# When a planner makes weight chunks ready around a layer norm, and when it keeps still

## The chip, the cores and the metric

The kernel runs on one core of one Trainium2 chip. The metric is device time in microseconds (us) of one execution. The time before the change is 2328.68 us, the median of three runs (2328.07 to 2328.75).

The engines are called as the profile calls them: PE is TensorE, the matrix engine; DVE is VectorE; ACT is ScalarE; SP is the queue of SyncE, which in this kernel does nothing but issue DMAs.

## The reference

One decoder layer in float32: batch 1, 256 tokens, model width 2048. Cut to what matters:

```python
h = x
h = layer_norm(alpha*h + 0.5 * swiglu(h, w_ffn1_gu, w_ffn1_down), ln_g[0], ln_b[0])

rq, rk, rv, rg, aq, ak, av, gate_r, gate_a = split(h @ w_in)
ret_branch = (silu(rg) * head_group_norm(retention(rotary(rq), rotary(rk), rv))) @ w_ret_out
att_branch = sliding_window_attention(rotary(aq), rotary(ak), av, sinks) @ w_att_out
mixed = (sigmoid(gate_r) * ret_branch + sigmoid(gate_a) * att_branch) @ w_mix_out
h = layer_norm(alpha*h + mixed, ln_g[1], ln_b[1])

h = layer_norm(alpha*h + 0.5 * swiglu(h, w_ffn2_gu, w_ffn2_down), ln_g[2], ln_b[2])

ple = sigmoid(h @ w_ple_gate) * (p @ w_ple_proj)
h = layer_norm(alpha*h + ple, ln_g[3], ln_b[3])
```

`swiglu(h, gu, down)` is `(silu(g) * u) @ down` with `g, u = split(h @ gu)` and an inner width of 5632. A layer norm needs all 2048 columns of a token before its mean and variance are known, so nothing that follows it can begin before the product ahead of it has ended for that token.

## The kernel before

**Products.** Every large product takes a high and a low part of both operands (`Sum.add`, L279 to L288): low x high, high x high and high x low are three matmuls into one PSUM bank. The activations lie transposed, contraction index on the partitions, high and low part of all 256 tokens in one tile (`ht`). The 256 tokens are two halves, t = 0 and t = 1, of 128 each.

**Weights.** Weights come in chunks of 512 KB (`Chunk`, L93). A chunk is loaded by one DMA from SP (L104), ACT casts its high part (L90), and DVE subtracts to get the low part (L91). These two together are called a split. A unit of the plan is either a `Single`, one chunk with 12 matmuls (2 halves of the tokens x 2 blocks of the contraction x 3), or a `Seven`, two chunks used in a Strassen-like form with 21 matmuls. All these tiles, and most other temporary ones (the norm's vectors among them), live in one pool of 46 slots (`slots`, L54) of 4 KB for each partition. A tile that is asked for takes the place of an earlier one, and the instruction that writes it first waits until the earlier tile's last reader is done.

**The planner.** The order of the instructions on each engine is the order in which the program writes them. `plan` is the list of all units in the order of use. `fill` (L183) goes on as long as it may: it makes the next loaded unit ready (the split) while the units that are ready sum up to less than `ahead` matmuls (45), and loads the next unit of the plan while ready and loaded ones sum up to less than `far` (90). Both need room within the number of slots last set by `slots_for_weights`. `take` hands out the next ready unit, `done` gives its slots back and calls `fill`. So a split stands on ACT and DVE at the point where the program called `fill`, ahead of all that the program writes later.

**Around a norm.** Three layer norms (i = 0 after the first feed-forward block, tile `f1y`; i = 1 after the mixers, `mixy`; i = 2 after the second feed-forward block, `f2y`) are handled by the class `Norm` (L484):

- `Norm.run` (L520) queues the four loads of the norm's vectors `ln_g` and `ln_b` (`ln_vectors`, L446; each 1024 values given to all 128 partitions, 512 KB). For i < 2 it also loads and splits `praw`, the per-layer input, into `pt` (L525 to L528). It then calls `held_out`.
- `held_out` (L394) goes over the last chunks before the norm twice. In the first pass it takes each chunk and multiplies it with the tokens of t = 0 only, calls `fill`, and keeps the chunk. Then `normal(0)` (L499) is written: DVE adds the last columns to the residual (`columns`, L494, L835 or L1184), works out mean and variance (`ln_stats`, L457), and normalizes the first 512 columns (`ln_normal`, L464, with its two instructions L468 and L469). In the second pass the kept chunks are multiplied with t = 1 on PE, while DVE normalizes t = 0. The argument `between` says after how many half chunks of the second pass the four groups of transposes (`turn`, L509, `ln_turn`, L471, the matmuls of L476) are written: (8, 9, 11, 12) for all three norms. ACT and DVE then make high and low part of each transposed group in the new `ht`; at norm 1, where `keepers` names two groups, ACT first copies these to `keep`, and they are split from there. Six chunks are held (`HELD_PAIRS` = 3 pairs of two columns, or `HELD_MIX` = 6).
- `Norm.first` (L549) belongs to the product behind the norm. The first six chunks (`FRONT`) of its weights are multiplied with t = 0 of the new activations, and meanwhile DVE normalizes t = 1 and PE transposes it, one group after the second, third, fourth and sixth chunk. Then the same six chunks are multiplied with t = 1. For the last product, `w_pg`, the groups stand after the fourth, fifth and sixth chunk with t = 0 and the second with t = 1. `first` calls `fill` after each chunk (L562) as well.
- For i < 2, `put_by` (L583) stands between the two: the product `pp` of the per-layer input, which doesn't need the norm's output.

The product behind norm 0 is `w_rv` (retention values), behind norm 1 the second feed-forward block's `f2_gu`, behind norm 2 `w_pg`.

## Time and profile before

| what | value |
| --- | --- |
| median of 3 runs | 2328.68 us (2328.07 to 2328.75) |
| the profiled execution's own time | 2328.84 us |
| its span, first to last instruction | 2327.1 us |
| mean granted clock of TensorE | 0.995 |
| busy: PE / DVE / ACT / POOL | 2289.2 / 1828.9 / 1145.5 / 96.6 us |
| read from HBM | 455.43 MB, 199 GB/s over the span |

The busy time of an engine is the time in which at least one of its counted instructions was under way. The span and the busy times are of one execution, whose own time is 0.16 us over the median. Two further kinds of view are used below. A list in order of time shows each instruction with its start, duration, engine, line, operation, out and in tiles, and in brackets the idle time of its engine ahead of it with what released it. The list of waits sums these idle times by place and releaser. Tiles are named as in the program, so `lnps` is the PSUM bank of the transposes, `lw_rv` the low part of a `w_rv` chunk, and `rw_`, `hw_` are the raw and the high tile of the same chunk.

### The profile page before, as it was taken

The numbers are of one execution on the slowest core, as the hardware profiler recorded it, in microseconds if no ns is written. First come the engines' busy times: TensorE is split into PE (matmuls) and PEld (weight loads), VectorE is DVE, ScalarE is ACT, GpSimd is POOL, SyncE is SP. The second block draws the span as 40 slices with busy tenths as digits, with TensorE's granted clock in tenths as the row PEclk, the third lists the DMA queues.
The fourth block names the chain that finished last, engine by engine and source line by source line (L and its number), as shares of the span: only waits on it lengthen the run. The fifth ranks groups of instructions, "written<-read, shape, count | busy, mean of one in ns | idle before, by whom it ended". The sixth has DMA issues, their size and how long they took to land.

```text
span 2327.1 us, 28608 instructions
## 1 busy us (share of the span) xinstructions
PE 2289.2 (98%) x10532; PEld 1893.4 (81%) x10532; DVE 1828.9 (79%) x2288; ACT 1145.5 (49%) x1384; POOL 96.6 (4%) x53
## 2 busy tenths in 40 slices
PE   9999999999998999999999999999999999999987
PEld 7888888888887888888778888788888888888876
DVE  7998988988987874777554555769898899889766
ACT  5655555555553343434554443355455555655432
POOL 0000000000000530133000000000000000000000
PEclk9999999999999999999999999999999999999998
DMA  9555665665586564545445666566566666465851
GB/s 316 188 192 186 210 205 171 208 211 193 197 304 239 172 223 160 171 157 189 163 155 181 199 210 215 193 233 211 181 197 201 190 196 219 168 222 199 332 192 55
DMA packets 193725, 465.71 MB, mean 200 GB/s; under 512 B 14768, under 2 KB 16048, under 8 KB 193584
## 3 DMA queue, kind: packets, MB, share of 16 engines
q1 hardware_dynamic: 191456, 460.91, 58.8%
q10 hardware_dynamic: 2128, 2.97, 0.4%
q8 instruction: 83, 1.36, 0.2%
q14 instruction: 58, 0.48, 0.1%
HBM read 455.43 MB, written 8.39 MB: 199 GB/s over the span
## 4 chain that ended last, share of the span: by engine, by line
PE 95%; DVE 4%; DMA 1%; issue 0%; ACT 0%; DVEq 0%; ACTq 0%
PE f1g L286 3%; PE f1g L288 3%; PE f1g L287 3%; PE f2g L286 3%; PE f2g L288 3%; PE f2g L287 3%; PE gt L286 3%; PE f1u L286 3%; PE f1u L288 3%; PE f1u L287 3%; PE rqk L237 3%; PE f2u L287 3%; PE f2u L288 3%; PE f2u L286 3%; PE gt L287 3%; PE gt L288 3%
## 5 line engine op out<-in xcount | busy, mean ns | idle before, releaser
L91 DVE TENSOR_TENSOR lf_gu<-rf_gu,hf_gu 128x1024 fp32r<-128x1024 f32 (+1 forms) x293 | 347.2, 1214 | 23.5 <-ACT hf_gu L90 22.6
L90 ACT CAST hf_gu<-rf_gu 128x1024 fp32r<-128x1024 f32 (+1 forms) x293 | 292.1, 1045 | 16.4 <-DMA rf_gu<-in_f_gu 12.5
L91 DVE TENSOR_TENSOR lw_in_f<-rw_in_f,hw_in_f 128x1024 fp32r<-128x1024 f32 x148 | 208.1, 1438 | 61.8 <-ACT hw_in_f L90 59.2
L91 DVE TENSOR_TENSOR lf_down<-rf_down,hf_down 128x1024 fp32r<-128x1024 f32 x152 | 179.7, 1219 | 20.2 <-ACT hf_down L90 16.8
L90 ACT CAST hf_down<-rf_down 128x1024 fp32r<-128x1024 f32 x152 | 154.5, 1050 | 68.4 <-DMA rf_down<-in_f_down 12.2
L90 ACT CAST hw_in_f<-rw_in_f 128x1024 fp32r<-128x1024 f32 x148 | 145.9, 1052 | 0.2
L90 ACT CAST huf_gu<-uf_gu 128x1024 fp32r<-128x1024 f32 x60 | 63.2, 1054 | 136.7 <-DVE uf_gu L163 133.4
L286 PE MATMUL f1g<-hf_gu,xt 128*128 128x512 f32 x262 | 103.2, 394 | 5.3 <-ACT hf_gu L90 5.3
L288 PE MATMUL f1g<-lf_gu,xt 128*128 128x512 f32 x262 | 102.9, 393 | 0.0
L287 PE MATMUL f1g<-hf_gu,xt 128*128 128x512 f32 x262 | 102.9, 393 | 0.0
L286 PE MATMUL gt<-hw_in_f,ht 128*128 128x512 f32 x256 | 102.5, 400 | 0.0
L286 PE MATMUL f2g<-hf_gu,ht 128*128 128x512 f32 x262 | 102.4, 391 | 0.0
L288 PE MATMUL f2g<-lf_gu,ht 128*128 128x512 f32 x262 | 102.0, 389 | 0.0
L287 PE MATMUL f2g<-hf_gu,ht 128*128 128x512 f32 x262 | 101.9, 389 | 0.0
L287 PE MATMUL gt<-hw_in_f,ht 128*128 128x512 f32 x256 | 99.9, 390 | 0.0
L288 PE MATMUL gt<-lw_in_f,ht 128*128 128x512 f32 x256 | 99.9, 390 | 0.0
L286 PE MATMUL f2u<-hf_gu,ht 128*128 128x512 f32 x232 | 91.5, 394 | 0.0
L286 PE MATMUL f1u<-hf_gu,xt 128*128 128x512 f32 x232 | 91.3, 394 | 0.0
L288 PE MATMUL f2u<-lf_gu,ht 128*128 128x512 f32 x232 | 90.8, 391 | 0.0
L287 PE MATMUL f2u<-hf_gu,ht 128*128 128x512 f32 x232 | 90.6, 391 | 0.0
L287 PE MATMUL f1u<-hf_gu,xt 128*128 128x512 f32 x232 | 90.3, 389 | 0.0
L288 PE MATMUL f1u<-lf_gu,xt 128*128 128x512 f32 x232 | 90.3, 389 | 0.0
(1053 smaller groups left out, 6070.9 us busy)
## 6 DMA issues: line engine op xcount, KB each, us to landing
rf_gu<-in_f_gu SPq DMA_DIRECT2D x351, 512.0 KB, 4.9
rf_down<-in_f_down SPq DMA_DIRECT2D x176, 512.0 KB, 4.5
rw_in_f<-in_w_in_f SPq DMA_DIRECT2D x148, 512.0 KB, 3.7
rw_rv<-in_w_rv SPq DMA_DIRECT2D x32, 512.0 KB, 5.0
rw_ret<-in_w_ret SPq DMA_DIRECT2D x32, 512.0 KB, 4.0
rw_mix<-in_w_mix SPq DMA_DIRECT2D x32, 512.0 KB, 4.3
rw_pg<-in_w_pg SPq DMA_DIRECT2D x32, 512.0 KB, 4.5
rw_att<-in_w_att SPq DMA_DIRECT2D x16, 512.0 KB, 4.2
```

The lines of the kernel that those rows point to most:

```text
L90: act.copy(dst_hi, src)
L91: (lo_engine or dve).tensor_tensor(dst_lo, src, dst_hi, ALU.subtract)
L237: pe.matmul(ps[f], hi[:, kk, f * P : (f + 1) * P], rhs(k), start=k == 0, stop=k == n_k - 1,)
L286: pe.matmul(o, al, bh, start=first, stop=False)
L287: pe.matmul(o, ah, bh, start=False, stop=False)
L288: pe.matmul(o, ah, bl, start=False, stop=self.left == 0)
```

## The change

The diff changes only how the planner works around the three norms, which chunks are held at the mixers' norm, and where the slot limits are set:

- `HELD_MIX` becomes 5, and the transposes at the mixers' norm are written after (8, 9, 10, 10) half chunks of the second pass.
- `fill` has a flag `quiet`: while it is on, nothing is made ready (loads go on), but for a `take` that finds nothing ready. `held_out` turns it on from the next to last held chunk of the first pass. `Norm.first` turns it off after the last group of transposes of t = 1.
- `slots_for_weights` also sets `ahead` and `far`. Before the held chunks `ahead` is raised to 160, 148 or 136 matmuls at the three norms and `far` to 184, 172 or 160, with 30 or 28 slots in place of 24. Each held chunk of the first pass lowers both by 12.
- The call `slots_for_weights(24)`, which stood at the beginning of the part behind each norm and now also brings back 45 and 90, moves behind `norm.first`.
- `held_out` for the very end of the kernel is told not to lower them (`calm` is False).

```diff
-HELD_MIX, HELD_END = 6, 8
+HELD_MIX = 5
...
-    room = {"slots": 0, "used": 0, "ahead": 45, "far": 90}
-
-    def fill():
+    room = {"slots": 0, "used": 0, "ahead": 45, "far": 90, "quiet": False}
+
+    def fill(must=False):
...
             left = room["slots"] - room["used"]
-            if loaded and queued < room["ahead"] and loaded[0].makes <= left:
+            wanted = must and not ready or not room["quiet"] and queued < room["ahead"]
+            if loaded and wanted and loaded[0].makes <= left:
...
     def take(key):
         if not ready:
-            fill()
+            fill(True)
...
-    def slots_for_weights(n):
-        room["slots"] = n
+    def slots_for_weights(n, ahead=45, far=90):
+        room.update(slots=n, ahead=ahead, far=far)
+
+    def quiet(on):
+        room["quiet"] = on
...
-    def held_out(steps, lhs, sums, of_columns, first_done, between):
+    def held_out(steps, lhs, sums, of_columns, first_done, between, calm=True):
...
             tokens_chunk(u.chunk, k0, lhs, [sums[t][n] for t in range(2)], (0,))
+            if calm:
+                room["ahead"] -= u.time
+                room["far"] -= u.time
+                quiet(j >= len(steps) - 2)
             fill()
...
                 hook(j + 1)
+                if j + 1 == max(turns):
+                    quiet(False)
...
                 hook(len(steps) + j + 1)
+                if len(steps) + j + 1 == max(turns):
+                    quiet(False)
+            quiet(False)
             self.put_away()
...
     def ffn(name, i, ht, norm, keep, residual, keepers, away):
-        slots_for_weights(6 if i == 0 else 24)
+        if i == 0:
+            slots_for_weights(6)
...
                 norm.first(steps, rhs, sums, (2, 3, 4, 6))
+                slots_for_weights(24)
...
-        def others(n):
-
-            slots_for_weights(SLOTS - 4 - n)
+        def others(n, ahead=45):
+
+            slots_for_weights(SLOTS - 4 - n, ahead, max(90, ahead + 12))
...
+        last_ahead = 160 if i < 2 else 136
...
-            others(4 + 2 * sum(at >= u for at in last.values()))
+            others(4 + 2 * sum(at >= u for at in last.values()), 45 if u < len(second) - 5 else last_ahead)
...
-        slots_for_weights(24)
+        slots_for_weights(30, last_ahead, last_ahead + 24)
         steps = [(down_keys(name, 1)(n, p), 2 * p, n) for n in range(2) for p in held]
...
     def mixers(ht, norm, residual, keepers, away):
-        slots_for_weights(24)
...
         norm.first([(("w_rv", 0, c), 2 * c, 0) for c in range(FRONT)], rhs, sums, (2, 3, 4, 6))
+        slots_for_weights(24)
...
         first = KD // 2 - HELD_MIX
+        slots_for_weights(28, 148, 172)
         for c in range(first):
...
-        slots_for_weights(24)
...
-        norm.run(steps, lhs, (8, 9, 11, 12))
+        norm.run(steps, lhs, (8, 9, 10, 10))
...
     def embedding(ht, norm, y):
-        slots_for_weights(24)
...
                 norm.first(steps, lhs, [[s] for s in sums], (4, 5, 6, 8))
+                slots_for_weights(24)
...
-            held_out(steps, lhs, [[s] for s in sums], lambda t, j: None, first_done, lambda n: None)
+            held_out(steps, lhs, [[s] for s in sums], lambda t, j: None, first_done, lambda n: None, False)
```

## The prediction

> **What bounds the kernel now.** I read first the page's busy times, then the list of what TensorE (PE) waited for, then the three norms in order of time.
>
> ```profile
> PE 2289.2 (98%) x10532; PEld 1893.4 (81%) x10532; DVE 1828.9 (79%) x2288; ACT 1145.5 (49%) x1384; POOL 96.6 (4%) x53
> ```
>
> PE is busy 2289.2 us (98% of the span). So only what makes PE wait, or slows its clock, can move the end.
>
> The waits of PE (line waited at, releaser: total us, times, longest):
>
> ```profile
> PE lnps L476 <- DVE f2y L469: 7.5, 7, 3.8
> PE lnps L476 <- DVE f1y L469: 6.4, 6, 2.6
> ...
> PE lnps L476 <- DVE mixy L469: 4.3, 5, 2.7
> ```
>
> Nearly all of PE's waiting is for the transposes of a normalized tile (L476), held by VectorE (DVE) finishing it (L469): 18.2 us over the three norms. Here is the first norm (f1y) on PE, then on DVE (start, duration, what, and in brackets the idle time before with its releaser):
>
> ```profile
> 700.79 0.39 PE L287 MATMUL f1e<-hf_down,f1ah 128*128 128x512 f32 x1
> ...
> 705.09 0.39 PE L288 MATMUL f1e<-lf_down,f1ah 128*128 128x512 f32 x1
> ...
> 709.62 0.66 PE L476 MATMUL lnps<-ident,f1y 128*128 128x128 f32 x4 [1.62 <-DVE f1y L469]
> ...
> 714.19 0.48 PE L286 MATMUL pp<-hw_pp,pt 128*128 128x512 f32 x1
> ...
> 722.46 0.60 PE L476 MATMUL lnps<-ident,f1y 128*128 128x128 f32 x4
> ...
> 727.05 0.66 PE L476 MATMUL lnps<-ident,f1y 128*128 128x128 f32 x4 [2.60 <-DVE f1y L469]
> ...
> 728.40 0.63 PE L286 MATMUL rv<-hw_rv,ht 128*128 128x512 f32 x1
> ...
> 728.83 0.63 PE L287 MATMUL rv<-hw_rv,ht 128*128 128x512 f32 x1
> ...
> 734.12 0.60 PE L476 MATMUL lnps<-ident,f1y 128*128 128x128 f32 x4
> ```
>
> ```profile
> 692.42 0.69 DVE L91 TENSOR_TENSOR pt<-praw,pt 128x512 fp32r<-128x512 f32 x1 [4.42 <-ACT pt L90]
> ...
> 696.78 0.68 DVE L835 TENSOR_TENSOR f1y<-f1y,f1e 128x512 f32<-128x512 f32 x1
> ...
> 698.10 1.21 DVE L91 TENSOR_TENSOR lw_pp<-rw_pp,hw_pp 128x1024 fp32r<-128x1024 f32 x1
> ...
> 701.50 0.68 DVE L835 TENSOR_TENSOR f1y<-f1y,f1e 128x512 f32<-128x512 f32 x1
> ...
> 702.94 0.26 DVE L459 BATCH_NORM_AGGREGATE mv<-f1st 128x2 f32<-128x24 f32 x1
> ...
> 704.89 0.48 DVE L468 SCALAR_TENSOR_TENSOR f1y<-f1y,mv,ln_g 128x256 f32<-128x256 f32 x1
> ...
> 720.92 4.62 DVE L91 TENSOR_TENSOR lw_rv<-rw_rv,hw_rv 128x1024 fp32r<-128x1024 f32 x4
> ```
>
> The second pass over the held chunks ends with the matmul at 705.09; four groups of transposes follow, with pieces of the second pass between them, and the next product starts at 714.19. In the second half of the tokens the four groups start at 722.46, 727.05 (after 2.60 us of waiting), 730.39 and 734.12. The 2.60 us come from the four splits at 720.92 (4.62 us), which stand on DVE ahead of the next normalization. Just after that wait matmuls start 0.43 us apart (728.40, 728.83), against (705.09 - 700.79)/19 = 0.226 us: the granted clock fell to half for a while. The second half took 734.12 - 722.46 = 11.66 us from first to last group.
>
> **The change, part by part.** The diff alone doesn't show the effect; I take the orders of the changed program's queues, and its waits, from the program as built. Matmuls, splits and loads keep their numbers. They move around three norms only; everywhere else the orders are the same.
>
> *(a) Splits moved from the second half to ahead of the first.* Four splits (rv chunks 2 to 5, gu pairs 1 and 2, pg chunks 4 and 5, with pg 6 and 7 and two of the next column block going behind) leave the place ahead of the second normalization, and the two between the later ones go behind all turns. Without waits and with the full clock, the four groups are 6, 6 and 12 matmuls apart. With about 0.36 us for four transposes, 0.31 for the matmul behind them and 0.226 for each further one, this gives 1.8 + 1.8 + 3.2 = 6.8 us. DVE keeps up: its four small normalizations end 6.8 us after the product starts (720.92 + 0.08 against 714.19), PE needs 36 matmuls, 8.2 us. Gain at norm 1: 11.66 - 6.8 = 4.9 us. The moved splits themselves cost nothing where they go if DVE has room: it sat idle for the 4.42 us before 692.42 among others.
>
> *(b) The constants of the norm are issued later.* This is the part that speaks against the change. `Norm.run` queues four 512 KB loads of the norm's vectors and the load `praw` on SyncE (SP) when it starts. In the changed program seven rv loads stand ahead of them on SP, all 46 slots are taken by then, and the five loads get slots that the held chunks leave only in their second pass:
>
> ```
> SP, changed, around norm 1 (slot freed by the second-pass matmul of)
> rw_rv_6  (held chunk 11, n=0)
> ln_g x2  (held chunk 20, n=0)
> ln_b x2  (a pp split; held chunk 21, n=0)
> praw     (held chunk 21, n=0, its last matmul)
> rw_rv_7  (held chunk 11, n=1)
> DVE, changed: ..., 4 rv splits, pt <- praw, columns (L835), statistics, normalize
> ```
>
> The split pt <- praw stands on DVE ahead of the columns (L835) and of everything that PE's first transposes need. Before, this load was issued at 682.84:
>
> ```profile
> 682.84 0.78 SPq L526 DMA_DIRECT2D praw<-in_pT  x1
> ...
> 691.76 0.62 ACT L90 CAST pt<-praw 128x512 fp32r<-128x512 f32 x1 [10.37 <-DMA praw<-in_pT]
> ```
>
> That a load goes out as soon as the releasing matmul ends can be seen at the last rv load, which waits for the matmul at 700.79 (end 701.18) today:
>
> ```profile
> 701.21 0.33 SPq L104 DMA_DIRECT2D rw_rv<-in_w_rv  x1
> ```
>
> The last matmul of held chunk 21, n=0 is the sixth before 705.09: start 703.73, end 704.12. Behind four vector issues of some 0.45 us (first at 702.55) praw goes out at 704.35. How long until it lands? The trace has it behind the same four vectors at the second norm:
>
> ```profile
> 1460.20 0.80 SPq L451 DMA_DIRECT2D ln_g<-in_ln_g  x2
> ...
> 1461.10 0.88 SPq L451 DMA_DIRECT2D ln_b<-in_ln_b  x2
> ...
> 1462.92 0.33 SPq L526 DMA_DIRECT2D praw<-in_pT  x1
> ```
>
> ```profile
> DMA to landing us min/median/max: 7.5/8.1/8.8
> ```
>
> 7.5 us there and 8.8 at the first norm, so I take 8.0 (first vector to landed praw: 9.3 to 10 us): landed at 712.3, bounds 711.8 to 713.2. Then, by rows: cast on ScalarE (ACT) 0.66 us after a start 0.1 later (691.76 to 692.42), pt 0.6, first columns 1.32 (696.78 to 698.10), second 1.44 (701.50 to 702.94), up to the normalization 1.95 (702.94 to 704.89). It starts at 718.4 instead of 704.89. Shift: 13.5 us, nearly all of it PE standing still, as it stands at 705.4 with nothing else queued.
>
> *(c) The clock after that stand.* PE is idle for some 13 us, so it resumes at half clock. Matmuls there wait for DVE anyway (the 1.62 us at 709.62 swallow some), so between 0.2 and 1.2 us remain; I take 0.7. The Trainium skill ("TensorE: Matmul & The Clock Gate", HAM oscillation) says that idle gaps over about 3.4 us bring half clock until a window of activity has passed. The 2.60 us wait above halved the clock too, so here the measurement is harsher than the page. By the page the next part's stall of 3.2 us would cost no clock, by the trace it may; that would make the sum 0.4 us smaller.
>
> Norm 1 in sum: +13.5 - 4.9 + 0.7 = **+9.3 us**.
>
> *(d) Second norm (mixy).* PE, then DVE:
>
> ```profile
> 1492.88 0.60 PE L476 MATMUL lnps<-ident,mixy 128*128 128x128 f32 x4
> ...
> 1507.53 0.60 PE L476 MATMUL lnps<-ident,mixy 128*128 128x128 f32 x4
> ...
> 1519.19 0.60 PE L476 MATMUL lnps<-ident,mixy 128*128 128x128 f32 x4
> ```
>
> ```profile
> 1480.97 2.35 DVE L91 TENSOR_TENSOR lw_pp<-rw_pp,hw_pp 128x1024 fp32r<-128x1024 f32 x2
> ...
> 1487.64 0.69 DVE L1184 SCALAR_TENSOR_TENSOR mixy<-mixy,mo 128x512 f32<-128x512 f32 x1 [2.04 <-PE mo L288]
> ...
> 1491.04 0.48 DVE L468 SCALAR_TENSOR_TENSOR mixy<-mixy,mv,ln_g 128x256 f32<-128x256 f32 x1
> ```
>
> Five chunks are held instead of six and the last two groups of transposes stand together at the end, so PE meets its first group six matmuls later, at 1492.88 + 1.36 = 1494.2. The vectors are issued when the third ordinary chunk is done (54 matmuls of both passes earlier, 1482.0), praw behind the second pp split: before these end at 1483.3, without pt ahead of them at 1482.7. So praw goes out at 1483.7 behind four vectors, on nearly idle DMA engines, and lands 9.5 us after the first vector: 1491.5 (bounds 1490.5 to 1492.5). Cast, pt and start of columns 1.4, then as before 3.40 (1487.64 to 1491.04): normalization at 1496.3, 5.2 us later than today, and with it the product behind. PE stalls some 3.2 us. The second half has 11.66 us today (1507.53 to 1519.19), 6.8 + 0.35 (the copies of `keep` make DVE late once) afterwards: -4.5. Half clock after the stall, two times in five: +0.4. Sum: **+1.1 us**.
>
> *(e) Third norm (f2y).* Here no praw is loaded, and the built program lets the vectors go once the last f2 down splits are made, about 2192; with 10 us they are there by 2202, and are needed at 2206. DVE, then PE:
>
> ```profile
> 2203.57 0.68 DVE L835 TENSOR_TENSOR f2y<-f2y,f2e 128x512 f32<-128x512 f32 x1
> ...
> 2223.00 4.62 DVE L91 TENSOR_TENSOR lw_pg<-rw_pg,hw_pg 128x1024 fp32r<-128x1024 f32 x4
> ```
>
> ```profile
> 2208.17 0.38 PE L476 MATMUL lnps<-ident,f2y 128*128 128x128 f32 x2
> ...
> 2222.22 0.44 PE L476 MATMUL lnps<-ident,f2y 128*128 128x128 f32 x2 [0.22 <-DVE f2y L469]
> ...
> 2229.22 0.63 PE L476 MATMUL lnps<-ident,f2y 128*128 128x128 f32 x4 [3.75 <-DVE f2y L469]
> ...
> 2236.10 0.60 PE L476 MATMUL lnps<-ident,f2y 128*128 128x128 f32 x4
> ```
>
> ```profile
> rw_pg<-in_w_pg SPq DMA_DIRECT2D x32, 512.0 KB, 4.5
> ```
>
> Splits pg 2 to 5 now stand ahead of the first columns. The last of their loads gets its slot from the 73rd matmul ahead of the transposes at 2208.17, at 2192.0; with the 4.5 us that pg loads take from issue to landing, 1 us of cast and 1.2 of split it is done by about 2199. So the second columns start when PE's first pass ends, 24 matmuls ahead of the transposes (2202.7), and not at 2203.57: -0.8, which runs through to the product behind the transposes. The second half lost 3.75 us of waiting to the splits at 2223.00 and the clock behind it: 13.88 us from 2222.22 to 2236.10, where 6.8 and the halves of the first group's wait (0.8) remain: -6.2. Sum: **-7.0 us**.
>
> *(f) What costs nothing:* the stores of y and the pp results move on SP behind some loads, and rv 6, 7 and what follows is split later. PE has 36 matmuls (8.2 us) of second pass before it needs rv 6; two splits are 2.4 us. If that cover failed, PE would wait for the difference, at most 2 us.
>
> **Sum:** +9.3 + 1.1 - 7.0 = +3.4 us on the profiled execution's 2328.84 us: 2332.2. The median of the runs is 2328.68, within 0.2 us of that execution; no correction.
>
> **The rivals.** 1. *Half clock for longer* (slower): the gate does not open while PE works in bits between DVE's steps, so transposes and the matmuls up to 3.4 us into pp run at half rate at norms 1 and 2. Price: 1.2 + 1.7 less the 0.7 counted, and 1.7 less 0.4: +3.5 us, 2335.7. For it: 3.5 us of half clock after a 2.60 us wait. Against: with half rate PE is busy nearly all of that time. It decides from 1.3 us on, since +4.7 is 0.2%. 2. *The change does what it seems to do* (faster): the late constants are hidden, through a quicker landing or because no wait holds them as I read it. Then -4.9 - 4.5 - 7.0 = -16.4 us: 2312.4. Against: 6 to 8 us from issue to landing on an issue that PE's second pass itself releases, with 1.3 us of PE work left. 3. *DVE late at the third norm as well*: a pg load takes 8.8 us, as praw did with the DMA engines full, instead of 4.5. Then the last split ends at 2203.2, the second columns start 1.3 behind it at 2204.5, 0.9 later than today: +1.7 against (e), 2333.9. Against: the issues of the changed program are spread there.
>
> **How the numbers follow.** My forecast 0.55, rival 1 0.22, rival 2 0.09, rival 3 0.14. The forecast's own range is 2329 to 2335, from the landing bounds (1 us at each of two norms) and the clock terms (1 us each). 0.2% is 4.7 us, about what a measurement can tell from no change. Slower: most of rival 1 (0.19), a third of rival 3 (0.05) and the forecast's upper tail (0.14), 0.38; faster: rival 2 and a little, 0.11; the same: 0.51. The range 2326.5 to 2338 leaves out rival 2 and the far ends.
>
> **What will show it.** In the changed profile: one wait of about 13 us at the transposes of f1y, released by DVE, with DVE idle before pt until praw lands near 712; a wait of about 3 us for mixy; the waits of 2.60, 2.67 and 3.75 us gone; the four groups of the second halves 7 us apart from first to last. I am wrong if praw is issued before 703 or lands before 709, if the wait at the first norm is below 10 us, if the second halves keep waits over 1 us, or if a wait shows up outside the norms.

## The result, and the profile after

The changed kernel takes 2336.8 us (median of 6 runs, 2335.82 to 2337.61) against 2328.72 us before (6 runs beside them): ratio 1.003, 95% interval 1.002 to 1.004. It is slower by 8.1 us, 0.35%, and a ratio of 1 lies outside the interval. The forecast was 2332.2 us in a range of 2326.5 to 2338.0: the time lies inside, 4.6 us above the predicted value. Of all executions reported here one, in the run with idle work, took 2568.62 us at a granted clock of 0.849; it is left out of that run's time and ratio.

The profiled execution took 2336.82 us, its span is 2335.0 us. The work is the same (PE busy 2289.3 us against 2289.2). What changed is the waiting. The waits of PE of the changed kernel (line waited at, releaser: total us, times, longest):

```profile
PE lnps L485 <- DVE f1y L478: 16.1, 3, 15.1
PE lnps L485 <- DVE mixy L478: 7.1, 4, 4.3
PE f1g L290 <- ACT hf_gu L90: 5.2, 1, 5.2
PE lnps L485 <- DVE f2y L478: 3.1, 4, 1.6
```

One wait of 15.1 us is new at the first norm and one of 4.3 us at the second. Those of 2.60, 2.67 and 3.75 us in the second halves are gone. The third line, `f1g`, is the very first block of the kernel waiting for its first weights. It stood in the list of before as well, so the norms had 18.2 of the 23.7 us of PE's waits there:

```profile
PE f1g L286 <- ACT hf_gu L90: 5.3, 1, 5.3
```

The first norm of the changed kernel, in order of time (start, duration, what, idle time before), on PE, DVE, ACT and SP:

```profile
704.82 0.39 PE L292 MATMUL f1e<-lf_down,f1ah 128*128 128x512 f32 x1
720.33 0.66 PE L485 MATMUL lnps<-ident,f1y 128*128 128x128 f32 x2 [15.12 <-DVE f1y L478]
...
726.97 0.63 PE L292 MATMUL f1e<-lf_down,f1ah 128*128 128x512 f32 x1
...
729.29 0.48 PE L290 MATMUL pp<-hw_pp,pt 128*128 128x512 f32 x1
...
737.59 0.60 PE L485 MATMUL lnps<-ident,f1y 128*128 128x128 f32 x4
...
744.46 0.60 PE L485 MATMUL lnps<-ident,f1y 128*128 128x128 f32 x4
```

```profile
701.00 1.23 DVE L91 TENSOR_TENSOR lw_rv<-rw_rv,hw_rv 128x1024 fp32r<-128x1024 f32 x1 [0.93 <-issue]
713.87 0.69 DVE L91 TENSOR_TENSOR pt<-praw,pt 128x512 fp32r<-128x512 f32 x1 [11.64 <-ACT pt L90]
...
719.18 0.48 DVE L477 SCALAR_TENSOR_TENSOR f1y<-f1y,mv,ln_g 128x256 f32<-128x256 f32 x1
```

```profile
713.22 0.62 ACT L90 CAST pt<-praw 128x512 fp32r<-128x512 f32 x1 [14.41 <-DMA praw<-in_pT]
```

```profile
691.41 10.07 SPq L104 DMA_DIRECT2D rw_rv<-in_w_rv  x4
702.29 0.80 SPq L460 DMA_DIRECT2D ln_g<-in_ln_g  x2
703.19 0.87 SPq L460 DMA_DIRECT2D ln_b<-in_ln_b  x2
704.16 0.70 SPq L535 DMA_DIRECT2D praw<-in_pT  x1
```

Read from the bottom: SP is held at the rv loads until 701.5 us, praw goes out at 704.16 and is there for ACT at 713.2. DVE has nothing to do for 11.64 us, then splits pt and only then starts the columns, so that PE stands from 705.2 to 720.3. After the stand matmuls start 0.43 us apart (duration 0.63), until about 728; the granted clock is 0.50 from 720 to 728 us. The second half takes 744.46 - 737.59 = 6.87 us, where it took 11.66.

The second norm, PE, then DVE and SP:

```profile
1509.08 0.44 PE L485 MATMUL lnps<-ident,mixy 128*128 128x128 f32 x2 [4.32 <-DVE mixy L478]
...
1516.32 0.80 PE L485 MATMUL lnps<-ident,mixy 128*128 128x128 f32 x4 [2.09 <-DVE mixy L478]
1516.78 0.78 PE L290 MATMUL pp<-hw_pp,pt 128*128 128x512 f32 x1
1517.35 0.63 PE L291 MATMUL pp<-hw_pp,pt 128*128 128x512 f32 x1
...
1526.63 0.60 PE L485 MATMUL lnps<-ident,mixy 128*128 128x128 f32 x4
...
1533.87 0.60 PE L485 MATMUL lnps<-ident,mixy 128*128 128x128 f32 x4
```

```profile
1504.02 0.69 DVE L91 TENSOR_TENSOR pt<-praw,pt 128x512 fp32r<-128x512 f32 x1 [4.13 <-ACT pt L90]
...
1508.02 0.48 DVE L477 SCALAR_TENSOR_TENSOR mixy<-mixy,mv,ln_g 128x256 f32<-128x256 f32 x1
```

```profile
1492.32 1.08 SPq L460 DMA_DIRECT2D ln_g<-in_ln_g  x2
...
1494.44 0.60 SPq L535 DMA_DIRECT2D praw<-in_pT  x1
```

And the third, PE:

```profile
2222.84 0.60 PE L485 MATMUL lnps<-ident,f2y 128*128 128x128 f32 x4
...
2225.74 0.66 PE L485 MATMUL lnps<-ident,f2y 128*128 128x128 f32 x4 [1.60 <-DVE f2y L478]
...
2236.26 0.44 PE L485 MATMUL lnps<-ident,f2y 128*128 128x128 f32 x2 [0.26 <-DVE f2y L478]
...
2244.05 0.60 PE L485 MATMUL lnps<-ident,f2y 128*128 128x128 f32 x4
```

For the comparison of runs I use three stages, each from the start of one matmul to that of another: the first norm from the first `f1e` to the first `rqk`, the second from the first `mo` to the first `f2d0s`, the third from the first `f2e` to the last `pg`. Between the stages the kernels run alike.

| stage, us | before | after | difference | predicted |
| --- | --- | --- | --- | --- |
| first norm | 748.2 - 593.8 = 154.4 | 758.5 - 593.5 = 165.0 | +10.6 | +9.3 |
| second norm | 2045.0 - 1407.6 = 637.4 | 2059.6 - 1417.9 = 641.7 | +4.3 | +1.1 |
| third norm | 2312.5 - 2096.6 = 215.9 | 2320.5 - 2111.3 = 209.2 | -6.7 | -7.0 |

With -0.3 us ahead of the first stage this is the +7.9 us of the spans (2335.0 - 2327.1). The stages of a run are those of its one profiled execution, whose time can lie up to 2.5 us from the median of the run (2335.96 and 2333.48 us with ahead 140).

### The profile page after: what moved, and what is told of

It is laid out like the page before. It is cut to its first block, busy times and chain, and to the rows that moved or that the text cites. A ratio compares the mean times of both kernels' runs of the same rounds, so it can differ in the third digit from the quotient of the medians.

```text
span 2335.0 us, 28611 instructions
## 1 busy us (share of the span) xinstructions
PE 2289.3 (98%) x10532; PEld 1896.1 (81%) x10532; DVE 1831.3 (78%) x2288; ACT 1148.0 (49%) x1384; POOL 96.6 (4%) x53
## 4 chain that ended last, share of the span: by engine, by line
PE 96%; DVE 2%; DMA 1%; ACT 0%; issue 0%; SPq 0%; DVEq 0%; ACTq 0%
PE f1g L290 3%; PE f1g L291 3%; PE f1g L292 3%; PE f2g L292 3%; PE f2g L291 3%; PE f2g L290 3%; PE gt L290 3%; PE f1u L290 3%; PE f1u L291 3%; PE f1u L292 3%; PE f2u L292 3%; PE f2u L291 3%; PE f2u L290 3%; PE rqk L241 3%; PE gt L291 3%; PE gt L292 2%
```

## The experiments

Theory: the constants of the norm (four vectors and praw) are queued late, pt is the first instruction on DVE that needs one of them, and everything up to PE's first transposes stands behind it; against that stand the gains of the second halves and of the third norm. Main rivals: DVE is late because of the splits that now stand ahead of the norm; or the half clock is the larger part.

All ratios are to runs of the kernel before on the same chip (medians 2328.88 to 2329.36 us).

### The split of pt behind the normalization

```diff
             if self.i < 2:
                 raw, pt = slot([P, 2, S], F32, "praw"), slot([P, 2, 512], F32R, "pt")
                 sync.dma_start(raw, io["pT"])
-                split(pt[:, :, :S], pt[:, :, S:], raw)
                 p_parts.append(pt)
...
+            def first_normal():
+                self.normal(0)
+                if self.i < 2:
+                    split(pt[:, :, :S], pt[:, :, S:], raw)
+
-            held_out(steps, lhs, self.sums, of_columns, lambda: self.normal(0), between)
+            held_out(steps, lhs, self.sums, of_columns, first_normal, between)
```

> The changed kernel with one edit: the split of the per-layer input (pt from praw) is written behind the first normalization of t = 0 and no longer ahead of its columns. The loads stay where the change put them, so praw still goes out last. Theory (the late constants stop DVE at pt, and with it the columns, the statistics and the normalization): columns and statistics now run while the constants are on their way, and the first normalization needs only the vectors. In the changed profile these go out at 702.29 and 703.19 us at the first norm and land 6.3 and 7.9 us later, so the second step of the normalization can start at 711.1 in place of 719.7. The pt split, with praw landing at 713.1, then holds the rest by about 2 us: -6.7 us at the first norm, about -7.5 at the second, 2322 us in all (2320 to 2325). Rival A (vectors and praw land together, the order on DVE doesn't matter): at most -2 us, 2335. Rival B (DVE is late because of the splits moved ahead, not of the constants): no change, 2336.8.

Measured: 2323.81 us, ratio 0.9979 (0.9971 to 0.9988), faster than before the change. The first stage is 158.2 us, 6.8 below the changed kernel, as expected; the second is 637.5, 4.2 below, where 7.5 was expected. The place of one split in the order of ACT and DVE is worth 13.0 us, with the loads and the six rv splits where the change put them, so neither the loads' place alone nor the number of splits makes the stall of 15.1 us. What is left of it are the late vectors themselves, for which DVE now waits inside the normalization (DVE, then PE):

```profile
711.46 0.48 DVE L478 SCALAR_TENSOR_TENSOR f1y<-f1y,rstd,ln_b 128x256 f32<-128x256 f32 x1 [2.16 <-DMA ln_b<-in_ln_b]
```

```profile
712.09 0.66 PE L485 MATMUL lnps<-ident,f1y 128*128 128x128 f32 x2 [6.48 <-DVE f1y L478]
```

Of the 3 us that are missing at the second norm 2.0 are half clock in pp (10.25 us from pp to the next group of transposes, 8.28 before the change), told below. The profiled execution took 2326.19 us, 2.4 us above the median of its run, so other executions may have had less of it.

### Constants queued ahead of the extra weights

```diff
+    def constants(i):
+        early["vectors"] = ln_vectors(i)
+        if i < 2:
+            early["raw"] = slot([P, 2, S], F32, "praw")
+            sync.dma_start(early["raw"], io["pT"])
...
-            self.vectors = ln_vectors(self.i)
+            self.vectors = early.pop("vectors")
...
+            if u == len(second) - 5:
+                constants(i)
+            n = 4 + 2 * sum(at >= u for at in last.values()) + (6 if u >= len(second) - 5 else 0)
-            others(4 + 2 * sum(at >= u for at in last.values()), 45 if u < len(second) - 5 else last_ahead)
+            others(n, 45 if u < len(second) - 5 else last_ahead)
...
-        slots_for_weights(30, last_ahead, last_ahead + 24)
+        slots_for_weights(25, last_ahead, last_ahead + 24)
...
-        slots_for_weights(28, 148, 172)
+        slots_for_weights(24, 148, 172)
         for c in range(first):
+            if c == 0:
+                constants(1)
```

> The changed kernel, but the four vector loads and praw are queued on SP ahead of the extra weight loads at the first norm and at the mixers' norm (five units before the end of the down projection, and ahead of the ordinary chunks of the last mixer block), and the slot limits there are lowered by six so that they find free slots. Raised ahead and far, quiet, five held chunks and the moved splits stay. At the third norm the vectors are moved forward in the same way. Theory: without the late constants both stalls (15.1 and 4.3 us) go, and what remains are the gains at the second halves and the third norm measured in the changed profile: -4.8, -4.4 and -6.7 on 2328.7 us: 2312.8 (2310 to 2316). Rival B (the splits ahead of the norm keep DVE late): at least half of the first stall stays, 2320 or more. Rival C (with fewer slots fewer chunks are ready, and waits come back in the second halves): 2316 to 2324, with waits of 1 to 3 us there.

Measured: 2331.13 us, ratio 1.0009 (1.0000 to 1.0018), far from 2312.8. The stages are 159.0, 638.1 and 209.9 us. A wait of 7.95 us stays at the first transposes, and the profile shows what is late: not praw, but the split of the fifth rv chunk, which stands on DVE just ahead of pt:

```profile
706.25 1.23 DVE L91 TENSOR_TENSOR lw_rv<-rw_rv,hw_rv 128x1024 fp32r<-128x1024 f32 x1 [5.28 <-ACT hw_rv L90]
```

DVE is idle for 5.28 us before it, because now this chunk's load has to wait for a slot (it goes out at 701.63, after SP has waited 10.9 us for a matmul). The place in the queue was mended, the pool of 46 slots was not: what came late was now the last of the weights made ahead. At the second norm no stall is left (its longest wait for transposes is 1.4 us), but with one gu pair less made ahead the second half waits again, 1.62 us for a cast alone. By its total (2320 or more), and with just over half of the first stall left, this is the outcome that rival B expected, in another form, and the theory and rival C have a part each: a split ahead of the norm hurts when its load is late.

### The third norm alone

The main edits against the kernel before (the flag `quiet` and the limit 24 behind the first product part come with them):

```diff
-            others(4 + 2 * sum(at >= u for at in last.values()))
+            others(4 + 2 * sum(at >= u for at in last.values()), 45 if i == 0 or u < len(second) - 5 else 136)
...
-        slots_for_weights(24)
+        slots_for_weights(24) if i == 0 else slots_for_weights(30, 136, 160)
...
-            held_out(steps, lhs, self.sums, of_columns, lambda: self.normal(0), between)
+            held_out(steps, lhs, self.sums, of_columns, lambda: self.normal(0), between, self.i == 2)
```

> The kernel before with the change at the third norm alone (raised ahead and far and quiet around it, slot limit 30, limit 24 set behind the first product part); the first two norms and the number of held chunks as before. Theory: the three norms are independent, and the third alone gives what lies between the two traces there, -0.6 us at its first half and -6.1 at its second: 2328.7 - 6.7 = 2322.0 us (2321 to 2323). Rival (part of that gain hangs on what the earlier norms do, or was noise of one profile): 2324 or more.

Measured: 2322.96 us, ratio 0.9974 (0.9963 to 0.9985). The third stage is 209.2 us, 6.7 below before, exactly as in the changed kernel. The third norm doesn't depend on what the change does at the other two, and the third term of the sum holds.

### Idle work in the stalls

```diff
+        for j in range({(0, 0, 0): 150, (1, 0, 0): 44}.get((i, t, k0), 0)):
+            pe.transpose(ps[:, j % nk, :], ident, ident)
```

> The changed kernel with idle work added: ahead of the first transposes of t = 0 PE transposes the identity 150 times at the first norm (some 13.4 us at 0.089 us each) and 44 times at the second (3.9 us) into the bank that the real transposes then overwrite. It fills the two stalls, so PE isn't idle for long before it resumes; nothing else moves. Theory with the clock as a small part (rival 1 of the prediction right at the second norm, where pp ran at half rate): -0.8 us at the first norm, -1 to -2.1 at the second: 2334.4 us (2333.9 to 2335.0), with matmuls 0.23 us apart right behind the stalls. If the clock had no part in it: 2336.8. If the half clock came from the later wait of 2.09 us at the second norm alone: -0.8 in all, 2336.0, and pp still at half rate.

Measured: 2336.06 us (median of five), ratio 1.0029 (1.0017 to 1.0041), between the theory and no effect. It is the number of the third alternative (2336.0), but not its sign, since pp does not run at half rate. The parts are clearer. The 150 transposes took 16.5 us (0.11 each) and end at the real ones. Behind them there is no half clock at either norm: from DVE's normalization to pp it is 730.21 - 720.91 = 9.30 us at the first norm, against 729.29 - 719.18 = 10.11 in the changed kernel. The 0.8 us are the price of the clock there, as predicted (0.7), but in this execution the normalization came later, because praw landed 10.2 us after its issue (704.65 to 714.9), and the stage is 165.5 us. The second stage is 639.1 us, 2.6 below the changed kernel. Of these, 1.6 us are pp at the full rate (8.29 us from pp to the next group, 9.85 in the changed kernel); the other 1.0 are not the clock's alone, since praw landed 1.5 us sooner there (7.3 us after its issue, 8.8 in the changed kernel) and the idle work ran 1.9 us past the normalization.

### Less made ahead

Two steps down in the amounts made ahead at the first two norms.

```diff
-        last_ahead = 160 if i < 2 else 136
+        last_ahead = 140 if i < 2 else 136
...
-        slots_for_weights(28, 148, 172)
+        slots_for_weights(28, 128, 152)
```

The second run has 128 in place of 140, and (28, 116, 140).

> The changed kernel with smaller amounts made ahead at the first two norms: ahead 140 and far 164 in place of 160 and 184 at the first, 128 and 152 in place of 148 and 172 at the second. Four rv chunks and two gu pairs are split ahead of the norm (six and three before), and SP queues the constants behind five rv loads (seven) and six gu loads, with slots that come free earlier: the vectors at the first norm wait for splits of the down weights (about 692 us in place of 702.3), praw for a matmul of the second pass at 701.3 (704.2). Theory (the stall is the lateness of the constants, so it shrinks with it): praw lands at about 707 in place of 713.1, the first stall falls from 15.1 to about 8 us, the second vanishes; the second halves lose about 2 us together to the splits that fall into them: 2326.5 us (2323 to 2330). Rival (the number of splits ahead of the norm makes DVE late, by 1.2 us each): two splits fewer save 2.4 us at each norm, 2332.

> As the run with ahead 140, one step further: ahead 128 and far 152 at the first norm, 116 and 140 at the second; three rv chunks and three gu chunks split ahead. At the first norm now all constants get slots from the first pass or from splits (at the latest about 692 us), at the second from the first ordinary chunk on. Theory: no stall at either norm (waits at the first transposes under 2 us), and the second halves lose 3 to 4 us together, with one to three splits among them: 2320 us (2317 to 2324), better than with 140, though less is made ahead. Rival (the splits made DVE late): another 1.2 us for each norm, 2330. Rival (second halves take back what was gained, as before the change): 2328.

Measured: 2333.48 us, ratio 1.0018 (1.0009 to 1.0027), and 2333.96 us, ratio 1.0022 (1.0013 to 1.0031). Both expectations of the total are missed (2330 and 2324 were the upper ends). For 140 the rival's total, 2332, is the nearer one, but the rows below do not bear out its mechanism. The first stage with 140 is 159.0 us, 6.0 less than in the changed kernel: the stall is 5.75 us, where the theory had about 8. With 128 it is 161.4: its stall of 4.92 us is not gone, since the fourth rv load holds SP until 692.5 and praw, out at 694.51 behind the four vectors, comes only at 703.7; and the second half gets three forced splits. At the second norm I had the costs wrong: with 140, praw is out at 1487.49 and there at 1496.4, a stall of 2.5 us stays, and the second half loses 1.62 + 0.71 us of waits and the full clock (stage 645.5 us); with 128 the stall is gone (longest wait 1.39 us), but the second half loses more (stage 641.5). It takes 12.1 us with 140 and 14.45 us with 128, where the changed kernel took 7.24.

What these runs settle is what the first transposes hang on as long as pt stands ahead of the columns. The split of pt and the first transposes at the first norm, with 140, with 128, and with the constants ahead (DVE and PE of each):

```profile
705.36 0.69 DVE L91 TENSOR_TENSOR pt<-praw,pt 128x512 fp32r<-128x512 f32 x1 [6.45 <-ACT pt L90]
```

```profile
711.83 0.66 PE L485 MATMUL lnps<-ident,f1y 128*128 128x128 f32 x2 [5.75 <-DVE f1y L478]
```

```profile
704.40 0.69 DVE L91 TENSOR_TENSOR pt<-praw,pt 128x512 fp32r<-128x512 f32 x1 [6.97 <-ACT pt L90]
```

```profile
710.86 0.66 PE L485 MATMUL lnps<-ident,f1y 128*128 128x128 f32 x2 [4.92 <-DVE f1y L478]
```

```profile
707.40 0.68 DVE L91 TENSOR_TENSOR pt<-praw,pt 128x512 fp32r<-128x512 f32 x1
```

```profile
713.86 0.66 PE L493 MATMUL lnps<-ident,f1y 128*128 128x128 f32 x2 [7.95 <-DVE f1y L486]
```

Transposes minus pt: 6.47, 6.46 and 6.46 us, and 720.33 - 713.87 = 6.46 in the changed kernel, with three, four, five or six rv splits ahead of pt. So in these four runs the first transposes follow pt at a fixed distance, and the number of splits does not change it. A split ahead of pt enters only where its own load is late, as with the constants ahead.

### Less ahead and pt behind the normalization

The two edits above together (ahead 140 and 128).

> The run with ahead 140, with the split of pt behind the first normalization as well. Theory: praw, the only constant that is late there, no longer holds the columns and the normalization, the vectors are in time: no stall above 2 us at either norm, with four rv chunks ready, so second halves between those of the changed kernel and of the run with 128: 2319 us (2316 to 2322). If vectors land late too: 2323 or more.

Measured: 2323.22 us, ratio 0.9975 (0.9966 to 0.9984), above the range by 1. The first stage is 151.4 us, 3.0 better than before the change: no wait for transposes above 2.2 us, and a second half with two forced splits. The second is 640.4 us, 3.0 worse than before, with the same 1.62 and 0.71 us of waits in the second half as with 140 and matmuls at half rate behind them for 5 us.

### Which of the two halves of the change does it: without quiet, and quiet alone

Without quiet, one line of the changed kernel goes:

```diff
             if calm:
                 room["ahead"] -= u.time
                 room["far"] -= u.time
-                quiet(j >= len(steps) - 2)
```

> The changed kernel without quiet: splits are allowed all the time, within the raised and falling ahead. By the order of DVE this moves rv chunks 6 and 7 ahead of the transposes of t = 1 at the first norm, gu chunk pairs ahead of and between them at the second, and pg 6 and 7 between them at the third. Theory: the late constants stay as they are (stalls of 15 and 4 us), and the second halves get waits back, about 2.4 us each at the first and second norm, 1 to 2 at the third: 2342 us (2339 to 2345). Rival (quiet does nothing that the lowered ahead doesn't do): 2336.8.

Quiet alone is the changed kernel with the amounts, limits and held chunks of before:

```diff
-        last_ahead = 160 if i < 2 else 136
+        last_ahead = 45
...
-        slots_for_weights(30, last_ahead, last_ahead + 24)
+        slots_for_weights(24)
...
-        slots_for_weights(28, 148, 172)
...
+        slots_for_weights(24)
         steps = [(("w_mix", 3, c), 2 * c, 0) for c in range(first, KD // 2)]
...
-                room["ahead"] -= u.time
-                room["far"] -= u.time
...
-HELD_MIX = 5
+HELD_MIX = 6
...
-        norm.run(steps, lhs, (8, 9, 10, 10))
+        norm.run(steps, lhs, (8, 9, 11, 12))
```

> The kernel before with quiet alone: nothing is made ready between the last two held chunks and the last transposes of t = 1, but for what PE takes next; amounts ahead, slot limits and held chunks as before (the limit 24 is set behind the first product part, as in the change). The constants keep their early place on SP. By the order of DVE all six rv chunks of the first norm, all gu chunks of the second and pg 2 to 5 at the third are then split one by one when PE needs them, between the transposes of the second half. Theory (the gain comes from splits being ahead of the norm, and quiet without them only moves them to where they hurt): second halves longer than before by 2 to 4 us each, 2337 us (2333 to 2342). Rival (quiet itself is what brings the gain, as splits no longer stand in one block): 2322 or less.

Measured: 2350.39 us, ratio 1.0090 (1.0076 to 1.0104), without quiet, and 2355.49 us, ratio 1.0112 (1.0096 to 1.0127), with quiet alone. Both signs were right, both sizes too small by more than the ranges allowed (8 and 18 us above my values). The third norm shows the pattern without late constants: 215.9 us before, 215.6 with the amounts alone, 222.1 with quiet alone, 209.2 with both. The waits of PE there, without quiet and with quiet alone:

```profile
2249.85 1.09 PE L484 MATMUL lnps<-ident,f2y 128*128 128x128 f32 x4 [4.18 <-DVE f2y L477]
```

```profile
2242.82 0.80 PE L292 MATMUL pg<-lw_pg,ht 128*128 128x512 f32 x1 [4.55 <-DVE lw_pg L91]
```

Without quiet the splits made next stand ahead of the normalization as before; with quiet alone PE waits for the splits themselves. Either half leaves the work of DVE in the second half or just ahead of it.

### praw ahead of the vectors

```diff
-            self.vectors = ln_vectors(self.i)
             if self.i < 2:
                 raw, pt = slot([P, 2, S], F32, "praw"), slot([P, 2, 512], F32R, "pt")
                 sync.dma_start(raw, io["pT"])
+            self.vectors = ln_vectors(self.i)
+            if self.i < 2:
                 split(pt[:, :, :S], pt[:, :, S:], raw)
                 p_parts.append(pt)
```

> The changed kernel with two steps exchanged: at the first two norms the load praw is queued ahead of the four vectors and not behind them. What was measured so far: behind four fresh vector loads praw landed 8.9 us after its issue (704.16 to 713.1), and 2.9 us after it where the vectors were already through (701.81 to 704.7, with ahead 140). Theory (the landing is the draining of what is queued before, so praw alone is quick): praw goes out at 702.3 and lands by about 706, pt ends at 707.3, and the first normalization waits for the last of its vectors, at about 712 in place of 719.2: -6.5 us at the first norm; at the second praw lands by 1496, DVE is free at 1500 and normalizes at about 1504 in place of 1508: -4 us. 2326 us (2323 to 2329). Rival (each landing takes 8 to 9 us whatever stands before it): pt at 712, -2 us at the first norm and -1 at the second, 2334.

Measured: 2327.59 us, ratio 0.9991 (0.9983 to 1.0000), within the theory's range and not the rival's. praw went out at 702.69 and was there at 708.0, 5.3 us later and not 8.9, but not by 706 as the theory had it. So pt still held the normalization, which came at 714.02 and not at 712, with no wait for the vectors. At the second norm praw landed 4.2 us after its issue, and pt waited for something else: ACT stood for 4.47 us until a matmul released it, probably for the slot of pt. The stages are 159.1, 638.0 and 209.2 us: -5.9 and -3.7 against the changed kernel. At the first norm pt runs at 708.70 and the first transposes at 715.16, again 6.46 us apart:

```profile
715.16 0.66 PE L485 MATMUL lnps<-ident,f1y 128*128 128x128 f32 x2 [9.56 <-DVE f1y L478]
```

So issuing praw ahead of the vectors, with everything else as in the change, gives back 9.2 us.

### Two combinations

The first takes the first norm of the run with ahead 140 and pt behind the normalization, the second norm as before the change, and the third as changed; the second combination keeps quiet and early splits at the second norm too, with six held chunks.

```diff
-        last_ahead = 160 if i < 2 else 136
+        last_ahead = 140 if i < 2 else 136
...
-HELD_MIX = 5
+HELD_MIX = 6
...
-        norm.run(steps, lhs, (8, 9, 10, 10))
+        norm.run(steps, lhs, (8, 9, 11, 12))
```

To these lines and the edit of pt come, in the first combination:

```diff
-        slots_for_weights(28, 148, 172)
...
+        slots_for_weights(24)
         steps = [(("w_mix", 3, c), 2 * c, 0) for c in range(first, KD // 2)]
...
-            held_out(steps, lhs, self.sums, of_columns, lambda: self.normal(0), between)
+            held_out(steps, lhs, self.sums, of_columns, first_normal, between, self.i != 1)
```

and in the second (30, 160, 184) in place of (28, 148, 172).

> A combination: first norm as in the run with ahead 140 and pt behind the normalization (151.4 us from the first f1e to the first rqk matmul there, against 154.4 before), second norm with amounts, limits, six held chunks and order of transposes as before the change (637.4 us from the first mo matmul to the first one of the second down projection), but pt behind the normalization, third norm as changed (-6.7 us). Theory (the norms add up): 2328.9 - 3.0 - 6.7 = 2319.2 us (2318 to 2321).

> As the combination, but the second norm with six held chunks, transposes after 8, 9, 11 and 12 half chunks, three gu pairs split ahead (ahead 160, far 184, limit 30), quiet, and pt behind the normalization. Theory: the constants are late there by no more than the second pass covers, since pt no longer holds the columns and there is one more held chunk, and the second half keeps the 4.4 us of the changed kernel, less 1 to 4 us for late vectors and half clock ahead of it: 2317 us (2315 to 2320). Rival (the half clock that two runs show there comes back with any set of small waits): 2319 to 2322, no better than the combination.

Measured: 2320.73 us, ratio 0.9961 (0.9949 to 0.9974), and 2323.14 us, ratio 0.9972 (0.9960 to 0.9983). The first lies in its range and beats both kernels, by 8.6 us the one before. Its stages are 151.5, 637.3 and 210.1 us, the first two as the sum had them, the third 0.9 above. The second lies above its range and above that of its rival (2319 to 2322). The rival's point holds: it is no better than the first, and half clock is back at the second norm behind waits of 1.80 and 0.48 us (matmuls of 0.63 us until 1499.9). Its profiled execution, with 638.0 us at that norm, is the fastest of the run (2320.79 us), so the median has lost 2.3 us more at a place that the profile doesn't show. The longest waits for transposes in the first combination are again those of the second half of the unchanged second norm (2.7 us) and of the first norm's first half (2.2):

```profile
PE lnps L485 <- DVE mixy L478: 4.2, 3, 2.7
PE lnps L485 <- DVE f1y L478: 2.9, 2, 2.2
```

## Why the prediction was right and where it was off

- **(a) Splits off the second half.** Right. The second halves took 6.87 and 1533.87 - 1526.63 = 7.24 us, against 6.8 and 7.15 predicted; gains of 4.8 and 4.4 us where 4.9 and 4.5 stood in the sum. That splits moved there cost nothing holds for the first two norms in the changed kernel, where DVE was idle for 11.64 and 4.13 us behind them, and is false as soon as one of their loads is late (the run with the constants ahead).
- **(b) Late constants.** Right in every step: praw out at 704.16 (predicted 704.35), DVE idle before pt, one wait of DVE's making at PE. The size was short: praw was there about 9 us after its issue, at the upper bound of the range and not at the 8.0 taken between two rows. The first normalization came at 719.18, predicted 718.4. How near the size comes is partly luck: at this place the same load, behind the same four vectors, took 8.8 to 10.2 us in the four runs that have the order of the changed kernel there. With praw first 3.6 of the 8.9 us are gone.
- **(c) The clock after the stand.** Right: 0.8 us at the first norm by the run with idle work (one profiled execution of each kernel), 0.7 predicted.
- **(d) Second norm.** The mechanism was right, the term mis-sized by 3.2 us, nearly all of the difference between forecast and result beside the 1.3 us of the first norm. With the 10.3 us by which this stage starts later taken off, praw went out at 1484.1 as predicted (1483.7), was there at 1493.0 (pt ran on DVE at 1504.02, 0.7 us behind it) and not at 1491.5, and the normalization came 6.65 us later than before, not 5.2: +1.4. From there to the start of pp another 0.6 us were lost, with half rate between the groups. The sum had no such wait as the 2.09 us ahead of the last group. And pp itself started at half rate behind it: from pp to the first group of the second half it took 1526.63 - 1516.78 = 9.85 us. Before, pp had this row:

```profile
1499.25 0.48 PE L286 MATMUL pp<-hw_pp,pt 128*128 128x512 f32 x1
```

  That made 1507.53 - 1499.25 = 8.28 us, so pp cost 1.6 us more, where 0.4 stood in the sum for the clock. So two steps failed: the landing, taken 1.1 us too short (7.8 us after the issue, where it took 8.9), and the half clock, given two chances in five and 0.4 us. The first rival was right here, and only here. Holding five chunks and writing the last two groups together was not tried alone, so its share at this norm is open.
- **(e) Third norm.** Right: -6.7 for -7.0. The second half takes 2244.05 - 2236.26 = 7.8 us in place of 13.88, -6.1 for -6.2; the remaining -0.6 (for -0.8) come ahead of it.
- **(f) What costs nothing.** Right in the changed kernel: no wait shows up for rv or gu chunks.
- **The rivals.** The second (constants hidden) and the third (third norm late) are out. The first holds at the second norm, and adds 1.2 of the 4.6 us that the forecast was short. Its number, 2335.7, is nearer than the forecast's, but not for its reason: at the first norm pp ran at full rate from its start. The time also lies above the forecast's own range, which ended at 2335, and inside the wider one that the rivals and their chances made. No measurable change, with 0.51 the likeliest, was wrong; slower had 0.38.

## What to carry to other kernels

When more work is queued ahead of a deadline, look first at what the same queue and the same pool carried there before: here seven weight loads pushed five loads of constants behind the last free slots, DVE met the late one first and stood for 11.6 us, and PE for 15.1. The operand that is needed first goes out first, and its consumer stands behind the work that doesn't need it; each repair moved one step and gave back 9 or 13 us. At the third norm early work and a quiet stretch paid only together, and at the first the run with the constants ahead shows the limit: slots for the early work must not be missing elsewhere.

## What the runs showed of the hardware that I had not expected

**The clock halves without any long gap.** With pt behind the normalization, the second norm has four short waits, none above 1.1 us, and pp still starts at half rate (0.63 us and 0.43 apart, until 1509.7):

```profile
1498.71 0.44 PE L485 MATMUL lnps<-ident,mixy 128*128 128x128 f32 x2 [0.20 <-DVE mixy L478]
...
1500.77 0.66 PE L485 MATMUL lnps<-ident,mixy 128*128 128x128 f32 x4 [0.91 <-DVE mixy L478]
...
1502.89 0.97 PE L485 MATMUL lnps<-ident,mixy 128*128 128x128 f32 x4 [0.76 <-DVE mixy L478]
1504.94 1.11 PE L485 MATMUL lnps<-ident,mixy 128*128 128x128 f32 x4 [1.09 <-DVE mixy L478]
...
1506.28 0.63 PE L291 MATMUL pp<-hw_pp,pt 128*128 128x512 f32 x1
...
1510.04 0.39 PE L291 MATMUL pp<-hw_pp,pt 128*128 128x512 f32 x1
```

The granted clock was 0.81 from 1500 to 1505 us and 0.51 from 1505 to 1510. With ahead 128 nearly the same waits (0.28, 0.96 and 1.39 us at the same place) left the clock at 1.00. So the length of one wait doesn't decide it, and I can't tell from these runs what does. The Trainium skill ("TensorE: Matmul & The Clock Gate", HAM oscillation) gives as its abstract rule that gaps above about 3.4 us are to be avoided; here the clock halved with no gap above 1.1 us, so gaps of that length aren't the only condition.

**How long it lasts varies too.** The run with the third norm alone has the first norm of before, instruction for instruction, and the same wait of 2.60 us. Yet its last two groups are 5.46 us apart, where 734.12 - 730.39 = 3.73 us were seen before:

```profile
727.14 0.66 PE L484 MATMUL lnps<-ident,f1y 128*128 128x128 f32 x4 [2.60 <-DVE f1y L477]
...
730.48 1.09 PE L484 MATMUL lnps<-ident,f1y 128*128 128x128 f32 x4 [0.79 <-DVE f1y L477]
...
735.94 0.60 PE L484 MATMUL lnps<-ident,f1y 128*128 128x128 f32 x4
```

Half rate lasted about twice as long (from 728.3 to 735.3 us, before from 728.0 to 731.5), which cost 1.7 us between these groups on the same code (stage 156.3 us in place of 154.4). Differences of that size at a single norm of a single profile aren't to be read as effects of an edit.

**A landing depends most on what is queued with it.** The same 256 KB of praw landed 6.9 to 10.2 us after its issue where four vectors of 512 KB had gone out in the 4 us before it (over all runs), 4.2 and 5.3 us where it went out just ahead of them, and 2.6 to 2.9 us where they had gone out more than 6 us earlier (701.81 to 704.7 with ahead 140). The spread among equal orders, 8.8 to 10.2 us at the first norm, has no explanation in these runs.
